# Cached keys transposed by VectorE in 32x32 blocks and scored on 16 array tiles, with a shared ring for keys, values and raw pieces

## The chip, the cores and the metric

The kernel runs on one core of one Trainium2 chip. The metric is the device time of one execution, in microseconds (us). The profile shows TensorE (PE; its weight loads are PEld), VectorE (DVE), ScalarE (ACT), GpSimd (POOL) and the queues of DMA that SP, ACT and GpSimd issue.

## The reference, cut to what matters

One layer of a hybrid decoder runs over a prompt of 256 tokens and over 8 samples of 8 new tokens each, all in float32 with 1024 features. Each sample has 1024 cached tokens in 8 pages of 128, found through a page table. The part that the change touches is the block-sparse attention of the samples: 4 heads of 128 features, blocks of 256 keys, and for each query the three past blocks with the highest mean score, beside the new tokens.

```python
h = x * (1.0 + scale) + shift
rq, rk, rv, rg, mq, mk, mv = project(h, w_in, pos)      # 1024 x 3072 columns, rotary on q and k
...
k_past = cache_k[page_table].reshape(dbs, past_len, h, d)   # 8 x 1024 x 4 x 128
v_past = cache_v[page_table].reshape(dbs, past_len, h, d)
...
gate = einsum("bqhd,bhnd->bqhn", q, kmean)              # mean key of each block of 256
_, top = lax.top_k(gate, 3)                             # of 4 past blocks
logits = einsum("bqhd,bqhsjd->bqhsj", q, ksel) * d ** -0.5
p = softmax(where(mask, logits, -inf))
out = einsum("bqhsj,bqhsjd->bqhd", p, vsel)
...
x = layer_norm(ALPHA * x + gate_a * (concat(retention, out) @ w_o))
x = layer_norm(ALPHA * x + gate_f * (relu(h2 @ w_up) ** 2 @ w_down))
```

## The kernel before

Weights and activations are split into a high and a low part, and a product is three matmuls of such parts. Weights come in pieces of [128, 1024] float32 (512 KB) into a ring of raw tiles, `wr`, of nine slots (`WR`); ScalarE makes the high part and VectorE the low one (`split1`, L162 and L164) into a second ring of eight, `wx`.

The work has three phases. The first, up to about 62 us, computes the modulation of the input by groups of 128 or 256 features (`ada_chunk0`, `pm`, L344) and with it the projection to q and k of the block-sparse heads (`zq`, L398 to L404). Five groups, `CH`, follow each other; the larger ones load four pieces of w_ada (`wa`) and two of w_in (`wi`), and `CUT` says how many units of a group's projection stand ahead of the next group's modulation.

The second phase is made of streams, each a generator whose steps a hand-written list, `SCHEDULE`, puts in an order: `mv`, `qk`, `rv`, `rg` (other columns of the projection), `ga`, `gs`, `gc` (three modulations, L510), `T`, `rT` (transposes of q and k), `K0` and `K1` (scores of the cached keys of samples 0 to 3 and 4 to 7), `V0` and `V1` (their weighted values), `h0` to `h3`, `rs`, `r0`, `r1`, `st`, `sr` (heads of the prompt and retention), `w..` (output projection), `n0` to `n2` (first norm), `ul`, `u0`, `us` (the feed-forward's first block). The list gives priorities; an instruction that waits in the planner's own model can be passed by a later one.

A step of `K0` gathers two pages of keys into a raw tile (`gather`, L267, on GpSimd's queue), transposes each page by heads on TensorE (L543, into the two banks tagged `k`), copies the result to SBUF (`kt`; L549 on ScalarE, L547 on VectorE) and scores pairs of pages with the queries that `pad_queries` has spread over 32 columns per head (L554, four tiles of 128x32 of the array; the scores of a group fill two banks, `psS`). `sample_softmax` chooses blocks and normalizes; `v_steps` loads pages of values, those of SP's queue through `page` (L284).

The third phase, from about 320 us, is the feed-forward by blocks of 512 features (`up`, L1052 to L1054; `down`, L402 to L404 into `acc`) and the second norm.

## Time and profile before

| what | value |
|---|---|
| time, median of 3 runs | 551.0 us (550.35 to 551.13) |
| the profiled execution: its span | 567.5 us |
| PE busy | 517.8 us (91%) |
| DVE, ACT, POOL busy | 311.1, 202.6, 152.8 us |
| data moved | 121.78 MB, mean 215 GB/s |

The span is that of one execution under the profiler, from its first instruction to its last; no other time of that execution is shown. The profiler's execution is longer than the timed ones. Busy time of an engine is the time in which at least one of its instructions of a group runs, so that groups which overlap count twice when added.

### The profile page before, as it was taken

Reading aid. Unit: us, or ns where it says so; the run is one execution under the profiler, and the core shown is the slowest. Engines: PE = TensorE matmul, PEld = TensorE weight load, DVE = VectorE, ACT = ScalarE, POOL = GpSimd, SP = SyncE. Lnnn points to the kernel's source line nnn. Section 1 sums busy time; section 2 is a strip of 40 time slices with the busy share of each in tenths; the row PEclk is TensorE's granted clock in tenths of the full one; section 3 lists DMA queues with packets and bytes.
Section 4 is the critical chain, followed back from the end, with each engine's and each line's share of the span. In section 5 each row is a group of like instructions: output and inputs, shape, how many; then the busy total and the mean of one; then the engine's idle time right before and its main releaser. Section 6 shows DMA issues by size and latency. Waiting matters only on the chain.

```text
span 567.5 us, 8901 instructions
## 1 busy us (share of the span) xinstructions
PE 517.8 (91%) x3346; PEld 398.6 (70%) x3346; DVE 311.1 (55%) x560; ACT 202.6 (36%) x332; POOL 152.8 (27%) x157
## 2 busy tenths in 40 slices
PE   4999999897986999899989888999999999999970
PEld 3777676665654657556658776989888898989860
DVE  1545864371254595573776779253635363636892
ACT  1324434131232533634353643252525252535200
POOL 3000235435572268572611076000000000000041
PEclk9999999999988999999989999899999999999995
DMA  8999978988593478979980645464554655340010
GB/s 219 350 363 371 320 259 284 327 294 323 184 301 127 150 251 287 348 277 317 362 301 2 224 184 164 170 220 153 185 187 167 213 173 175 109 151 1 1 55 37
DMA packets 55364, 121.78 MB, mean 215 GB/s; under 512 B 5321, under 2 KB 18209, under 8 KB 55322
## 3 DMA queue, kind: packets, MB, share of 16 engines
q1 hardware_dynamic: 46954, 97.56, 50.2%
q0 software_dynamic: 7424, 22.75, 11.9%
q10 hardware_dynamic: 944, 0.92, 0.5%
q8 instruction: 26, 0.43, 0.3%
q14 instruction: 16, 0.13, 0.1%
HBM read 117.33 MB, written 3.87 MB: 214 GB/s over the span
## 4 chain that ended last, share of the span: by engine, by line
PE 80%; DVE 7%; another core or an unknown queue 3%; DMA 2%; ACT 2%; issue 2%; POOL 1%; ACTq 0%; SPq 0%; POOLq 0%; DVEq 0%
PE pu L1052 7%; PE pu L1054 6%; PE pu L1053 6%; PE pk L543 5%; PE acc L402 4%; PE acc L403 4%; PE acc L404 4%; PE po L647 3%; PE psS L554 3%; PE acc L399 3%; PE acc L398 3%; PE pm L344 2%; DMA wa<-in_w_ada_dram 2%; PE pw L402 1%
## 5 line engine op out<-in xcount | busy, mean ns | idle before, releaser
L267 POOL DMA_INDIRECT kp<-in_cache_k_dram,idx x64 | 65.9, 1030 | 112.3 <-DMA ga<-in_w_ada_dram 50.9
L996 POOL TENSOR_TENSOR l22r<-l22r,mhalf 64x1 f32<-64x1 f32 x1 | 0.5, 542 | 186.5 <-DVE l22r L995 186.5
L549 ACT ACTIVATE kt<-pk 128x512 f32<-128x512 f32 x48 | 27.9, 596 | 43.7 <-PE pk L543 15.9
L1152 DVE TENSOR_TENSOR usq<-relu 128x320 f32<-128x320 f32 x32 | 17.6, 554 | 45.2 <-ACT relu L1147 44.0
L543 PEld LDWEIGHTS pk<-ident,kp 128*128 128x128 f32 x256 | 28.4, 140 | 18.1 <-issue 12.0
L543 PE MATMUL pk<-ident,kp 128*128 128x128 f32 x256 | 39.0, 280 | 1.1 <-issue 0.8
L1147 ACT ACTIVATE relu<-pu 128x320 f32<-128x320 f32 x28 | 12.1, 432 | 51.6 <-PE pu L1054 51.6
L547 DVE COPY kt<-pk 128x512 f32<-128x512 f32 x16 | 11.0, 690 | 33.0 <-PE pk L543 15.5
L554 PE MATMUL psS<-kt,qpad 128*32 128x256 f32 x256 | 22.4, 388 | 4.7 <-issue 2.4
L184 ACT ACTIVATE uT<-usq 128x320 fp32r<-128x320 f32 x32 | 15.0, 470 | 21.6 <-DVE usq L1152 21.6
L267 POOL DMA_INDIRECT v<-in_cache_v_dram,idx x16 | 18.5, 1157 | 12.1 <-PE po L647 4.5
L187 DVE TENSOR_TENSOR uT<-usq,uT 128x256 fp32r<-128x256 f32 x32 | 15.7, 490 | 7.9 <-ACT uT L184 7.5
L647 PE MATMUL po<-v,PT 128*32 128x512 f32 x128 | 18.1, 601 | 0.0
L344 PE MATMUL pm<-wa,cT 128*32 128x128 f32 x256 | 13.5, 293 | 4.7 <-DMA wa<-in_w_ada_dram 4.7
L344 PEld LDWEIGHTS pm<-wa,cT 128*32 128x32 f32 x256 | 10.0, 117 | 8.5 <-issue 4.5
L1129 POOL TENSOR_TENSOR x<-x,lng 128x512 f32<-128x512 f32 (+1 forms) x6 | 10.1, 1704 | 21.4 <-DMA lng<-in_ln_g_dram 21.4
L554 PEld LDWEIGHTS psS<-kt,qpad 128*32 128x32 f32 x256 | 6.4, 108 | 12.1 <-issue 7.0
L909 POOL TENSOR_TENSOR sg<-sg,rge 128x256 f32<-128x256 f32 (+1 forms) x6 | 4.4, 732 | 23.3 <-DVE rge L907 20.0
L908 DVE RECIPROCAL rge<-rge 128x256 f32<-128x256 f32 (+1 forms) x6 | 10.5, 1743 | 0.1
L1130 POOL TENSOR_TENSOR x<-x,lnb 128x512 f32<-128x512 f32 (+1 forms) x6 | 9.9, 1675 | 0.0
L188 DVE TENSOR_TENSOR uT<-usq,uT 128x64 fp32r<-128x64 f32 x32 | 9.2, 287 | 0.0
L1037 ACT ACTIVATE h2T<-px,shT,scT 128x128 fp32r<-128x128 f32 x16 | 7.0, 458 | 5.2 <-DVE h2f L1038 3.8
(1381 smaller groups left out, 1609.3 us busy)
## 6 DMA issues: line engine op xcount, KB each, us to landing
up<-in_w_up_dram SPq DMA_DIRECT2D x32, 512.0 KB
dn<-in_w_down_dram SPq DMA_DIRECT2D x32, 512.0 KB
v<-in_cache_v_dram SPq DMA_DIRECT2D x48, 256.0 KB
wa<-in_w_ada_dram SPq DMA_DIRECT2D x16, 512.0 KB
wi<-in_w_in_dram SPq DMA_DIRECT2D x8, 512.0 KB
ga<-in_w_ada_dram SPq DMA_DIRECT2D x8, 512.0 KB
gs<-in_w_ada_dram SPq DMA_DIRECT2D x8, 512.0 KB
gc<-in_w_ada_dram SPq DMA_DIRECT2D x8, 512.0 KB
```

The source lines that it names most:

```text
L267: nc.gpsimd.indirect_dma_start(out=dst, out_offset=None, in_=table, in_offset=bass.IndirectOffsetOnAxis(ap=idx[:, b * NPG + s:b * NPG + s ...
L344: pm_last.append(nc.tensor.matmul(pm[32 * j:32 * j + 32, 0:128], cT[:, k, :], wa[c, j // 2, k // per][:, k % per, 128 * i:128 * i + 128], ...
L402: nc.tensor.matmul(acc, hi, wh, start=first, stop=False)
L403: nc.tensor.matmul(acc, lo, wh, start=False, stop=False)
L404: nc.tensor.matmul(acc, hi, wl, start=False, stop=last)
L543: nc.tensor.transpose(pk[:, 128 * h:128 * h + 128], kp[:, s, 128 * h:128 * h + 128], ident)
L549: nc.scalar.activation(dst, src, AF.Copy)
L554: nc.tensor.matmul(psS[pr // 2][32 * h:32 * h + 32, c], qpad[:, h, 4 * g + b, :], kt[:, h, :], start=(b == 0 and pr % 2 == 0), stop=(b == ...
L647: nc.tensor.matmul(po[32 * b:32 * b + 32, :], PT[:, b, s, :], vt[b // 2][:, b % 2], start=False, stop=(s == NPG - 1), skip_group_check=True)
L1052: nc.tensor.matmul(pu[:, toks], wh, hi, start=first and k == ks[0], stop=False)
L1053: nc.tensor.matmul(pu[:, toks], wl, hi, start=False, stop=False)
L1054: nc.tensor.matmul(pu[:, toks], wh, lo, start=False, stop=last and k == ks[-1])
```

## The change

Keys are gathered by four pages into a tile of 1 MB and transposed in place by VectorE, each page of [128, 512] by one instruction in blocks of 32x32. A block then has 32 features in partitions and 32 keys in columns, so that the scores are products over 32 partitions: 16 tiles of the array work side by side, four by groups of keys (each with a bank of its own, four banks instead of two) and four by heads, and four products over blocks of features add up to a head's score. The queries are transposed the same way and copied to four groups of partitions (`pad_queries`, now once for each half of the samples). The softmax first adds the choice of blocks on VectorE into an SBUF tile in the order of keys, then takes one exponential.

Slots change: the raw ring has four instead of nine, a new ring of three tiles of 1 MB (`kv`, opened after the first phase) serves keys, values, and two pieces at a time of the feed-forward's weights and parts; `kt` goes. PSUM's banks are split seven and one instead of six and two. `SCHEDULE` has a new order: keys go with `mv`, `qk`, `rv`, `rg`, and the modulations `ga`, `gs`, `gc` go with the values. The diff, cut to its core:

```diff
-T mv*2 T qk ga T ga mv ga*2 mv qk T mv T qk T mv K0 mv ga mv tb mv K0 ga*2 mv qk mv ga qk mv K0
...
+T*2 K0*3 mv*3 T mv T mv K0 T mv T mv K0*2 mv*2 K0*2 mv*3 tb K0*2 qk*2 ok K0*2 qk*2 ok K0*2 qk*3 K0 qk*2 ov K0 qk*3 ov
+K0 rv*2 K1*3 rv*2 K0 ro rv*2 K1 rv*2 ro K1*2 rv*2 rT K1*2 rv*2 ro K1*2 rT rg*2 K1*2 rg*3 rT K1*2 rg*3 K1 rg*2 K1 rg*2
+K1 sw*2 V0*2 ga rs mx sw V0 ga rs K1 sw h0 V0 ga h1 sw V0 ga*2 r0 sw h0 V0 ga h1 r0 h2 V0 ga sr h3 ga gs r1 h0 V0 gs h2
...
-    WR, WX = 9, 8
+    WR, WX = 4, 8
-        return ps.tile([128, 512], F32, tag=tag, name=nm, bufs={"z": 6, "k": 2}[tag])
+        return ps.tile([128, 512], F32, tag=tag, name=nm, bufs={"z": 7, "k": 1}[tag])
...
+            two = halves(f"{nm}r", self.shape) if kv else ()
+            self.raw = [load(two[i] if i < len(two) else raw_tile(f"{nm}{i}", self.shape),
...
+    def kv_tile(nm):
+        return kvp.tile([128, 4, 512], F32, tag="kv", name=nm, bufs=3)
...
+    qpad = mid.tile([128, 16, 4, 32], F32, tag="qp", name="qpad")
+    def pad_queries(g):
+        if not qtr:
+            qtr[0] = t = mid.tile([64, 512], F32, tag="gny", name="qtr", bufs=1)
+            nc.vector.transpose(t, zs[2][:, 0:512])
+        for r in range(4):
+            v = qpad[32 * r:32 * r + 32]
+            dst = bass.AP(tensor=v.tensor, offset=v.offset, ap=[list(v.ap[0]), [128, 16], [40, 4], [1, 8]])
+            src = qtr[0][32 * g:32 * g + 32].rearrange("p (c b q) -> p c b q", c=16, b=4)
+            if r % 2:
+                nc.gpsimd.tensor_copy(dst, src)
+            else:
+                nc.scalar.activation(dst, src, AF.Copy)
...
-                for h in range(4):
-                    nc.tensor.transpose(pk[:, 128 * h:128 * h + 128], kp[:, s, 128 * h:128 * h + 128], ident)
...
+        def keys(b, half):
+            kt = kv_tile(f"k{g}{b}{half}")
+            for s in range(4):
+                gather(kt[:, s], ck_rows, 4 * g + b, 4 * half + s)
+                nc.vector.transpose(kt[:, s], kt[:, s])
+            return kt
+        def scores(b, half, kt):
+            for j in range(4):
+                for h in range(4):
+                    for r in range(4):
+                        p = slice(32 * r, 32 * r + 32)
+                        nc.tensor.matmul(psS[r][32 * h:32 * h + 32, 128 * half:128 * half + 128],
+                                         qpad[p, 4 * h + j, b, :], kt[p, :, 128 * h + 32 * j:128 * h + 32 * j + 32],
...
+        for r in range(4):
+            v = P[:, 32 * r:32 * r + 32]
+            dst = bass.AP(tensor=v.tensor, offset=v.offset, ap=[list(v.ap[0]), [256, 4], [128, 2], [1, 32]])
+            nc.vector.tensor_tensor(dst, psS[r][:, 0:256].rearrange("p (n s l) -> p n s l", n=4, s=2),
+                                    be[:, :, None, None].to_broadcast([128, 4, 2, 32]), op=ALU.add)
+        nc.scalar.activation(P[:, 0:1024], P[:, 0:1024], AF.Exp, bias=nmx, scale=QS, accum_out=sm[:, 0:1])
...
-                if b % 2 == 0:
-                    vt.append(raw_tile(f"v{g}{s}{b}", [2, 512]))
-                page(vt[b // 2][:, b % 2], 4 * g + b, s)
+                page(vt[:, b], 4 * g + b, s)
...
+        psS = [bank(f"psS{g}{r}") for r in range(4)]
+        if g:
+            pad_queries(1)
...
-        return Weights(wup[0], f"up{blk}", 0, 8, 512 * blk, 512)
+        return Weights(wup[0], f"up{blk}", 0, 8, 512 * blk, 512, kv=True)
...
-            pu = bank("pu", "k")
+            pu = bank("pu", "kz"[m % 2])
```

## Rows read from the trace of the kernel before

**Rows 1.** The page's head and first part: busy us, share, instructions.

```profile
span 567.5 us, 8901 instructions
...
PE 517.8 (91%) x3346; PEld 398.6 (70%) x3346; DVE 311.1 (55%) x560; ACT 202.6 (36%) x332; POOL 152.8 (27%) x157
```

**Rows 2.** Windows by stage: columns as the head line says.

```profile
core 0: us, PE busy (x) PEld busy (x) DVE busy (x) ACT busy (x) POOL busy (x), PEclk, DMA share, GB/s
...
62.00:184.00 122.00, 109.30 (x747) 73.47 (x747) 57.48 (x90) 34.12 (x56) 54.66 (x62) 0.96 0.78 270
184.00:320.00 136.00, 129.31 (x882) 85.98 (x881) 89.03 (x202) 61.53 (x122) 60.04 (x56) 0.99 0.71 246
320.00:567.50 247.50, 225.78 (x1275) 198.17 (x1274) 135.62 (x201) 86.89 (x128) 29.95 (x21) 0.96 0.42 144
```

**Rows 3.** The chain of waits by line, its head.

```profile
by line: PE pu L1052 6.6%; PE pu L1054 6.5%; PE pu L1053 6.3%; PE pk L543 5.4%; PE acc L402 4.0%; PE acc L403 3.9%; PE acc L404 3.9%; PE po L647 3.2%; PE psS L554 2.9%; another core or an unknown queue 2.6%; PE acc L399 2.6%; PE acc L398 2.
```

**Rows 4.** Groups by line: busy us, mean ns; idle before, releaser.

```profile
L543 PE MATMUL pk<-ident,kp 128*128 128x128 f32 x256 | 39.0, 280 | 1.1 <-issue 0.8 <-ACT kt L549 0.3
L549 ACT ACTIVATE kt<-pk 128x512 f32<-128x512 f32 x48 | 27.9, 596 | 43.7 <-PE pk L543 15.9 <-issue 10.6 <-remote 8.1
L554 PE MATMUL psS<-kt,qpad 128*32 128x256 f32 x256 | 22.4, 388 | 4.7 <-issue 2.4 <-DVE kt L547 2.3
...
L547 DVE COPY kt<-pk 128x512 f32<-128x512 f32 x16 | 11.0, 690 | 33.0 <-PE pk L543 15.5 <-remote 8.2 <-issue 5.0
...
L613 DVE TENSOR_SCALAR P<-P,rs 128x1088 f32<-128x1088 f32 x2 | 1.6, 788 | 0.1
```

**Rows 5.** TensorE's waits, 62 to 320 us: total, times, longest.

```profile
PE psS L554 <- issue: 2.4, 3, 1.2
PE psS L554 <- DVE kt L547: 2.3, 2, 1.6
```

**Rows 6.** Timeline of TensorE and its weight loads: start us, us.

```profile
28.23 1.94 PE L344 MATMUL pm<-wa,cT 128*32 128x128 f32 x60
...
100.17 0.16 PEld L554 LDWEIGHTS psS<-kt,qpad 128*32 128x32 f32 x8 [0.17 <-issue]
...
L554 PEld LDWEIGHTS psS<-kt,qpad x256: 106/109/110, 94.1 to 248.8; 128*32 128x32 f32 x128
```

**Rows 7.** The chain of waits, 64 to 90 us: start us, us.

```profile
83.17 1.00 PE gap L510 x16
88.58 0.57 PE gap L510 x8
```

**Rows 8.** Loads and splits: SP's and VectorE's timeline, the chain's DMA.

```profile
22.77 6.76 SPq L174 DMA_DIRECT2D wa<-in_w_ada_dram  x4
...
26.31 1.22 DVE L164 TENSOR_TENSOR wi10l<-wi,wi10h 128x1024 fp32r<-128x1024 f32 x1
...
351.00 3.48 DMA g<-in_w_ada_dram
```

**Rows 9.** Groups by line within 62 to 184 us, TensorE.

```profile
L543 PE MATMUL pk<-ident,kp 128*128 128x128 f32 x132 | 20.5, 280 | 0.8 <-issue 0.8
L554 PE MATMUL psS<-kt,qpad 128*32 128x256 f32 x128 | 11.7, 386 | 3.4 <-DVE kt L547 2.3 <-issue 1.1
...
L510 PE MATMUL gsp<-gs,cT 128*32 128x256 f32 x64 | 5.5, 389 | 0.0
```

**Rows 10.** GpSimd's timeline, two gathers of 256 KB behind each other.

```profile
129.86 0.95 POOL L267 DMA_INDIRECT kp<-in_cache_k_dram,idx  x1 [0.30 <-issue]
131.12 0.95 POOL L267 DMA_INDIRECT kp<-in_cache_k_dram,idx  x1 [0.31 <-issue]
```

**Rows 11.** DMA from 62 to 320 us; windows of 80 and 20 us.

```profile
DMA packets 27258, 66.35 MB, mean 257 GB/s; under 512 B 3390, under 2 KB 5490, under 8 KB 27235
...
60.00:140.00 80.00, 73.97 (x516) 50.74 (x515) 42.53 (x58) 23.33 (x34) 32.83 (x36) 1.00 0.89 311
...
300.00:320.00 20.00, 17.61 (x127) 15.73 (x126) 14.39 (x24) 9.31 (x15) 1.81 (x2) 1.00 0.14 44
```

More of the change, by code (lines that the diff above doesn't have):

```diff
@@ L138, in tile_decoder_step, with __init__ @@
     class Weights:
-        def __init__(self, w, nm, r0, nk, c0, ncol, slots=()):
+        def __init__(self, w, nm, r0, nk, c0, ncol, slots=(), kv=False):
             self.slots = list(slots)
@@ L144, in __init__ @@
             self.nm, self.shape = nm, [self.per, ncol]
-            self.raw = [load(raw_tile(f"{nm}{i}", self.shape), kview(w, r0 + 128 * self.per * i, self.per, c0, ncol))
-                        for i in range(nk // self.per)]
+            two = halves(f"{nm}r", self.shape) if kv else ()
+            self.raw = [load(two[i] if i < len(two) else raw_tile(f"{nm}{i}", self.shape),
+                             kview(w, r0 + 128 * self.per * i, self.per, c0, ncol)) for i in range(nk // self.per)]
             self.parts = {}
@@ L156, in part @@
             def part(x):
-                pl, tag, bufs = self.slots.pop(0) if self.slots else (wpool, "wx", WX)
+                slot = self.slots.pop(0) if self.slots else (wpool, "wx", WX)
+                if callable(slot):
+                    return slot(x)
+                pl, tag, bufs = slot
                 return pl.tile([128] + self.shape, F32R, tag=tag, name=f"{self.nm}{i}{x}", bufs=bufs)
@@ L472, in tile_decoder_step @@
     px1.close()
+    kvp = ctx.enter_context(pool("kvp", side="right"))
     pR = ExitStack()
@@ new lines, in kv_tile, with halves, kv_parts, slot @@
+    def kv_tile(nm):
+        return kvp.tile([128, 4, 512], F32, tag="kv", name=nm, bufs=3)
+    def halves(nm, shape, dtype=F32):
+        v = kvp.tile([128, 2] + shape, dtype, tag="kv", name=nm, bufs=3)
+        return v[:, 0], v[:, 1]
+    def kv_parts(nm, shape):
+        both = {}
+        def slot(x):
+            if not both:
+                both.update(zip("hl", halves(nm, shape, F32R)))
+            return both[x]
+        return [slot, slot]
+    qpad = mid.tile([128, 16, 4, 32], F32, tag="qp", name="qpad")
@@ new lines, in tile_decoder_step @@
+    nc.gpsimd.memset(qpad, 0.0)
+    qtr = {}
+    def pad_queries(g):
[10 more added lines that the diff above has]
+                nc.scalar.activation(dst, src, AF.Copy)
@@ new lines, in k_steps @@
+    def k_steps(g, psS):
+        def keys(b, half):
[11 more added lines that the diff above has]
+                                         qpad[p, 4 * h + j, b, :], kt[p, :, 128 * h + 32 * j:128 * h + 32 * j + 32],
+                                         start=(b + half + j == 0), stop=(b == 3 and half == 1 and j == 3),
+                                         skip_group_check=True)
+        late = []
@@ L560, in k_steps @@
         for b in range(4):
-            for pr in range(4):
-                one, scores = transposes(b, pr)
-                one(0)
+            for half in range(2):
+                late.append((b, half, keys(b, half)))
                 yield
-                if late:
-                    late.pop()()
-                one(1)
-                yield
-                late.append(scores)
-        late.pop()()
-        yield
+                if len(late) > 2:
+                    scores(*late.pop(0))
+                    yield
@@ L573, in tile_decoder_step @@
+        for a in late:
+            scores(*a)
+            yield
     PTs = []
@@ L862, in qk_T @@
             if t == 2:
-                pad_queries()
+                pad_queries(0)
             yield
@@ L912, in values @@
     def values(g):
-        po = bank(f"po{g}", "zk"[g])
+        po = bank(f"po{g}")
         yield from v_steps(g, PTs[g], po)
@@ L918, in scores @@
     def scores(g):
-        psS = [bank(f"psS{g}{hf}") for hf in range(2)]
+        psS = [bank(f"psS{g}{r}") for r in range(4)]
+        if g:
+            pad_queries(1)
         yield from k_steps(g, psS)
@@ L1017, in norm1 @@
         for gq in range(8 // per):
-            px = bank("px2", "k")
+            px = bank("px2")
             for q in range(per):
@@ L1075, in up0_sample @@
     def up0_sample():
-        p = bank("us", "k")
+        p = bank("us")
         for k in range(8):
```

68 lines of the change are left out of this document (18 added, 50 removed).

## The prediction

> **What bounds the kernel now.** I read the page first, then its windows by stage, the chain of waits, and the groups by line. The page's first part shows TensorE busy for 91% of a span of 567.5 us [rows 1]. An average over stages says little, so the windows come next: in 62 to 184 us, TensorE works 109.3 of 122 us while VectorE works 57.5 and the DMA engines 78%; in 184 to 320 us it is 129.3 of 136; from 320 us on the feed-forward alone runs [rows 2]. So in the stage that the change touches, TensorE ends last nearly everywhere, and the other three have room. The chain of waits agrees: it is TensorE's lines throughout, and the keys' transposes (L543) and their scores (L554) hold 5.4% and 2.9% of it [rows 3]. That is 30.6 + 16.5 = 47.1 us of 567.5. The reader should compare this with the groups by line, where the same two lines have 39.0 and 22.4 us busy [rows 4]: overlapping work counts twice there, and I use the chain. TensorE's own waits for this stream add little: 2.4 + 2.3 us [rows 5].
>
> The profiled execution shows its span only, 16.5 us above the median of 551.0. I sum changes of the span and take them off 551.0 one to one.
>
> **What is removed.** The 256 transposes and 256 score records leave the chain: -47.1 us, and the waits for copies of keys -4.7 us. ScalarE loses 48 copies of keys (27.9 us) and VectorE 16 (11.0 us) [rows 4]. Neither stands on the chain as a long piece, so I count nothing for them; what would have shown is VectorE's and ScalarE's slack, and VectorE's is spent below.
>
> **The new scores on TensorE.** The old code has 128 score products and the trace has 256 records [rows 4]: one f32 product is two records. The new code has 1024 products of 32 rows by 32 columns over 128 moving columns, so 2048 records, in 16 batches. Nothing in the trace runs 16 tiles. The nearest row is the modulation's first product, also 32 columns wide and 128 columns long on four tiles: 60 records in 1.94 us, so about 31 ns each [rows 6]. At that price the scores cost 64 us. Is that a limit of the array or of issuing? The batches of 256 columns tell: 16 records take 1.00 us of the chain and 8 take 0.57 [rows 7], so 8 more cost 0.43, 54 ns each. Twice the columns cost nearly twice the time, so it is the array's four tiles and not the issue that sets 31 ns. Sixteen tiles would make it a quarter, 7.8 ns, and 16 us in all; with the fixed 0.14 us of a batch (0.57 - 0.43) 16 times, 18 us. So the ends are 18 and 64 us. I take 24, near the low end, because eight weight loads of about 109 ns each were over after 0.16 us [rows 6], so they started some 7 ns apart; and a third above it, because no stretch shows 128 such records behind each other.
>
> On this the Trainium skill speaks against the change: "TensorEngine Tiling (Array Packing)", section Instruction Overhead, gives each matmul about 60 cycles whatever its columns. By that page, as an estimate, 2048 records cost at least 51 us at 2.4 GHz, and the sum below would end slower than before. The starts 7 ns apart disagree with it for a burst of eight; no row here shows a long run of such records.
>
> **The ring of raw pieces, nine slots to four, in the first 62 us.** The shared ring of keys and values opens only after this phase, so here nothing replaces the five slots. A group of features has four pieces of w_ada and two of w_in. With nine slots SP issues the next group's w_ada at 22.77 us, before TensorE reaches it at 28.23 [rows 6, 8]. With four, the last piece of that group takes the slot of a w_in piece, which comes free with its split, at 26.31 + 1.22 = 27.5 us [rows 8]. A load of 512 KB took 3.48 us where it was waited for [rows 8]: it lands near 31 instead of before 28.2, so some 2.5 us late. The two groups behind repeat the pattern, with part of the delay already absorbed; I count 1.25 us each: +5 us in all. The bounds are 0 (the loads, fewer at once, land sooner) and 4 groups x 3.5 = 14 us.
>
> **VectorE, GpSimd and the queues in the stage of keys and projections.** The new order puts all keys beside mv, qk, rv and rg, and moves the three modulations (5.5 us on TensorE each) behind them. In 62 to 184 us TensorE's work becomes 109.3 less the part of the keys there (20.5 + 11.7) less 3 x 5.5 plus 24: about 85 us [rows 2, 9]. VectorE's becomes 57.5 - 11.0 + 64 transposes. A transpose of 128x512 f32 isn't in the trace; the nearest row is the copy of the same size, 690 ns [rows 4]. The bounds are 0.37 us (half of the 788 ns that one operand of 1088 columns takes within SBUF [rows 4]) and 1.22 us (two operands of 1024 columns [rows 8], were it to run at half speed). At 0.69 they cost 44 us and VectorE comes to 91, plus about 2 for the softmax (four additions of 256 columns at half of 0.69 us, more and shorter reductions). GpSimd issues a gather every 1.25 us [rows 10]: 64 of them are 80 us. So VectorE, at 93, passes TensorE by 8 us, with GpSimd close behind; the transposes stand in VectorE's queue with the splits of the weights, and whoever waits for a late gather there holds up the splits that TensorE needs. I add 8 us for the longer engine and 2 for single steps: the one bank left for transposes, the copies of padded queries ahead of the gathers on GpSimd. +10 us; bounds 0 (at 0.37 us VectorE is at 72, far below TensorE) and, at 1.22 us a transpose, 10 + 34.
>
> **Cross-check by DMA.** From 62 to 320 us 66.35 MB moved, and the best 80 us of that had 311 GB/s [rows 11]. The smaller ring leaves about five slots' worth, 2.6 MB, more to do. 69 MB at 311 GB/s are 222 us; from 67 us on that ends at 289, and about 18 us without loads follow, as at 300 to 320 us now (44 GB/s) [rows 11]. That gives 307 us for the end of the stage instead of 320. The new kernel needs the best rate of the old one throughout, so there is little behind this sum to gain.
>
> **Costed at nothing.** In the feed-forward ten half-megabyte pieces (four slots and three pairs) stand for nine, its TensorE is 225.8 of 247.5 us busy [rows 2], and its loads run far ahead. If that cover fails, a load waited for costs 3.5 us per block. The values come in tiles of four pages instead of two of two, three tiles ahead of their use, with the same products. The order of mixing, heads and retention changes, but not their number of instructions.
>
> **The sum.** -47.1 - 4.7 + 24 + 5 + 10 = -13 us: 551.0 - 13 = 538 us.
>
> **The rivals.**
> - *All of it is gained* (0.13). Scores at 18 us, no queue in front of VectorE, loads keep up: -47.1 - 4.7 + 18 + 5 = -29, so 522 us, and 514 if the ring too costs nothing and the loads run ahead. For it: 16 tiles should run at a quarter of 31 ns. Against it: it needs a DMA rate over 311 GB/s for the whole stage.
> - *TensorE issues too slowly for 16 tiles* (0.20), the case on the other side. Its place is the batch of 128 records, its price 2048 times the distance of two starts. All else as in my sum, the change breaks even where the scores cost 37 us, 18 ns a record, and gets slower from there. At 31 ns, the only sustained row, it is -47.1 - 4.7 + 64 + 5 + 10 = +27, 578 us; the middle is 564. For it: no long run of short records is shown. Against it: the 7 ns between weight loads. The rule of "TensorEngine Tiling (Array Packing)" in the Trainium skill points to this case.
> - *VectorE takes TensorE's place* (0.17). With transposes between 0.69 and 1.22 us, or with gathers late in front of them, the stage is 13 to 34 us longer than I count: 551 to 572 us, middle 560. For it: four resources within 80 to 93 us in one stage and queues that run in order. Against it: VectorE is busy for only 47% of that window now.
> - *The time stays* (0.08). Loads, not TensorE, set the stage's end; with 295 GB/s, a little under the best, 69 MB take 234 us, and 67 + 234 + 18 = 319: 550 us. For it: the old order mixes loads and work more evenly. Against it: DMA is 78% busy and has room.
> - My forecast has 0.42, with a range of its own from 527 to 548 us.
>
> **How the numbers follow.** The likeliest time is 538 us. The range from 514 to 566 leaves out the upper halves of the second and third rivals (0.10 and 0.07) and the lowest corner of the first (0.03). The bound for no change is 0.2%, 1.1 us, about what three runs can tell. Faster gets my forecast, the first rival and a little of the third, 0.57; the same 0.07; slower 0.36.
>
> **What would show it.** Right: the lines L543 and L549 gone; 2048 records of scores with 1.0 to 1.8 us for a batch of 128; transposes on VectorE near 0.69 us; the last group of the first phase some 5 us later; TensorE's waits in the stage now for VectorE or DMA. Wrong: a batch over 2.3 us, transposes over 1 us, the first phase late by over 10 us, or a feed-forward longer than 247 us.

## The result, and the profile after

The changed kernel takes 628.0 us (median of 4 runs, 625.2 to 630.3) against 550.7 us measured beside it: 1.140 times the time before, 95% interval 1.136 to 1.144. The forecast of 538 us was wrong in sign, and no rival came near either: the longest time that I gave one was 578 us. The profiled execution is the longest of the four runs (630.25 us, span 628.5), so profiling need not lengthen an execution, as I had written of the one of before. That one stood 16.5 us above its median; in the groups of runs below the kernel before took medians of 550 to 573 us, and which execution its trace was is not on record. So the spans differ by 61 us and the medians by 77; the stages below account for the 61.

The page's head and first part, after:

```profile
span 628.5 us, 11849 instructions
...
PE 532.6 (85%) x4882; PEld 402.1 (64%) x4882; DVE 344.5 (55%) x626; ACT 178.2 (28%) x277; POOL 160.9 (26%) x161
```

Against [rows 1], TensorE is busy for 15 us more although 256 transposes are gone, and its busy share falls from 91% to 85%. Where the time lies is read from the ends of four things on TensorE: the last product of the first phase (zq), of w_o (pw), of the first block's sample rows (usT), and the end. The windows between them, after, and the one of before for the second:

```profile
core 0: us, PE busy (x) PEld busy (x) DVE busy (x) ACT busy (x) POOL busy (x), PEclk, DMA share, GB/s
76.00:327.00 251.00, 220.79 (x3019) 138.06 (x3018) 155.62 (x314) 56.08 (x93) 110.86 (x113) 0.96 0.76 255
...
327.00:364.00 37.00, 24.79 (x153) 22.46 (x154) 23.27 (x45) 16.73 (x31) 5.15 (x5) 0.77 0.33 108
364.00:628.50 264.50, 230.06 (x1265) 198.41 (x1264) 136.74 (x201) 86.10 (x128) 30.17 (x21) 0.96 0.39 131
```

```profile
62.00:300.00 238.00, 221.00 (x1502) 143.72 (x1502) 132.12 (x269) 86.33 (x164) 112.89 (x117) 0.97 0.79 275
```

| stage | before | after | difference | forecast |
|---|---|---|---|---|
| first phase, to zq | 62 | 76 | +14 | +5 |
| keys, values, to w_o | 238 | 251 | +13 | -18 (-47.1 -4.7 +24 +10) |
| norm and first block | 20 | 37 | +17 | 0 |
| feed-forward | 247 | 264 | +17 | 0 |

No stage gained. In the one with the keys TensorE is busy as long as before, 221 us of both, and idle for 13 us more. The +13 is less sure than the others: three traces of the changed kernel have 251, 249 and 263 us in this stage (a_again and a_again2 below). The last is from a group in which before took 564 us, the level nearest to the trace of before; against it the four differences are +13, +25, +17 and +17. The groups by line that answer to [rows 4], the values' products before, and the chain's loads of the first phase:

```profile
L570 DVE STREAM_TRANSPOSE k<-k 128x512 f32<-128x512 f32 x64 | 43.4, 698 | 35.3 <-DMA k<-in_cache_k_dram,idx 35.1
L578 PE MATMUL psS<-k,qpad 32*32 32x128 f32 x2048 | 40.0, 297 | 6.6 <-issue 2.7 <-ACT qpad L562 2.0 <-POOL qpad L560 1.6
L672 PE MATMUL po<-v,PT 128*32 128x512 f32 x128 | 29.3, 632 | 0.7 <-DMA v<-in_cache_v_dram 0.7
```

```profile
L647 PE MATMUL po<-v,PT 128*32 128x512 f32 x128 | 18.1, 601 | 0.0
```

```profile
30.37 3.45 DMA wa<-in_w_ada_dram
40.42 4.85 DMA wa<-in_w_ada_dram
...
55.70 6.58 DMA wa<-in_w_ada_dram
```

The transposes cost what was expected (698 ns, 43.4 us). The scores hold TensorE for 40.0 us and let it wait 6.6 more, instead of 24. The values' products stretch from 18.1 us to 29.3 with the same 128 records: eight of them took 3.04 us at 230.5, where before eight took 1.07 at 224.8; four of them run side by side when the pages of four samples are there, and one by one when the pages land so. And w_ada's loads, of which only the first stood on the chain of this phase before, are now on it again and again. The head of the chain of waits for the keys' stage, 76 to 327 us:

```profile
by line: PE psS L578 9.7%; DMA k<-in_cache_k_dram,idx 8.5%; issue 7.3%; PE po L672 5.1%; POOL k L270 4.8%; DMA wo<-in_w_o_dram 3.6%; DMA gc<-in_w_ada_dram 2.7%; DMA v<-in_cache_v_dram 2.2%; PE pw L407 2.2%; SPq L286 2.1%; DVE rge L933 2.1%;
```

The loads of keys, w_o, gc and values are on it with 8.5, 3.6, 2.7 and 2.2%. In the same stage before, no load stands among its first lines by name, but 6.2% are an unknown queue, two waits of 7 us; [rows 3] has it too, and the prediction passed over it:

```profile
by line: PE pk L543 12.9%; PE po L647 7.6%; PE psS L554 7.0%; another core or an unknown queue 6.2%; PE pw L402 3.6%; PE pw L404 3.4%; PE pw L403 3.1%; PE pns L826 2.4%; issue 2.1%; PE gap L510 2.0%; PE gcp L510 1.8%; PE mvz L402 1.6%; PE r
```

TensorE's waits over the whole span, after:

```profile
PE pm L347 <- DMA wa<-in_w_ada_dram: 14.1, 9, 2.9
PE g3p L1219 <- DMA g<-in_w_ada_dram: 10.5, 6, 5.1
PE pu L1081 <- POOL h2T L1067: 7.8, 1, 7.8
```

### The profile page after: what moved, and what is told of

The parts are those of the page before. It is cut to its first block, busy times and chain, and to the rows that moved or that the text cites. A ratio compares the mean times of both kernels' runs of the same rounds, so it can differ in the third digit from the quotient of the medians.

```text
span 628.5 us, 11849 instructions
## 1 busy us (share of the span) xinstructions
PE 532.6 (85%) x4882; PEld 402.1 (64%) x4882; DVE 344.5 (55%) x626; ACT 178.2 (28%) x277; POOL 160.9 (26%) x161
## 4 chain that ended last, share of the span: by engine, by line
PE 52%; DVE 15%; DMA 15%; issue 6%; POOL 5%; ACT 3%; SPq 2%; POOLq 0%; DVEq 0%; ACTq 0%
PE pu L1079 6%; PE pu L1081 5%; DMA wa<-in_w_ada_dram 5%; PE pu L1080 5%; PE psS L578 4%; DMA k<-in_cache_k_dram,idx 3%; PE acc L405 3%; PE acc L406 3%; PE acc L407 3%; DMA g<-in_w_ada_dram 3%; POOL k L270 3%; PE acc L402 2%; PE acc L401 2%; PE po L672 2%; PE pm L347 2%
## 5 line engine op out<-in xcount | busy, mean ns | idle before, releaser
L270 POOL DMA_INDIRECT k<-in_cache_k_dram,idx x64 | 69.5, 1086 | 104.8 <-ACT wi41h L165 56.9
L570 DVE STREAM_TRANSPOSE k<-k 128x512 f32<-128x512 f32 x64 | 43.4, 698 | 35.3 <-DMA k<-in_cache_k_dram,idx 35.1
L578 PE MATMUL psS<-k,qpad 32*32 32x128 f32 x2048 | 40.0, 297 | 6.6 <-issue 2.7
L578 PEld LDWEIGHTS psS<-k,qpad 32*32 32x32 f32 x2048 | 29.1, 107 | 17.4 <-issue 7.7
L672 PE MATMUL po<-v,PT 128*32 128x512 f32 x128 | 29.3, 632 | 0.7 <-DMA v<-in_cache_v_dram 0.7
L347 PE MATMUL pm<-wa,cT 128*32 128x128 f32 x256 | 16.2, 341 | 14.1 <-DMA wa<-in_w_ada_dram 14.1
L347 PEld LDWEIGHTS pm<-wa,cT 128*32 128x32 f32 x256 | 11.8, 138 | 19.0 <-DMA wa<-in_w_ada_dram 12.4
L190 DVE TENSOR_TENSOR uT<-usq,uT 128x256 fp32r<-128x256 f32 x32 | 16.8, 524 | 2.6 <-ACT uT L187 1.6
L270 POOL DMA_INDIRECT v<-in_cache_v_dram,idx x16 | 16.0, 997 | 6.4 <-issue 5.1
L1219 PE MATMUL g3p<-g,cT 128*32 128x256 f32 x64 | 6.0, 452 | 10.6 <-DMA g<-in_w_ada_dram 10.5
L672 PEld LDWEIGHTS po<-v,PT 128*32 128x32 f32 x128 | 4.4, 110 | 11.9 <-issue 5.8
```

The costliest lines, as they stand in the source:

```text
L270: nc.gpsimd.indirect_dma_start(out=dst, out_offset=None, in_=table, in_offset=bass.IndirectOffsetOnAxis(ap=idx[:, b * NPG + s:b * NPG + s ...
L347: pm_last.append(nc.tensor.matmul(pm[32 * j:32 * j + 32, 0:128], cT[:, k, :], wa[c, j // 2, k // per][:, k % per, 128 * i:128 * i + 128], ...
L570: nc.vector.transpose(kt[:, s], kt[:, s])
L578: nc.tensor.matmul(psS[r][32 * h:32 * h + 32, 128 * half:128 * half + 128], qpad[p, 4 * h + j, b, :], kt[p, :, 128 * h + 32 * j:128 * h + ...
L672: nc.tensor.matmul(po[32 * b:32 * b + 32, :], PT[:, b, s, :], vt[:, b], start=False, stop=(s == NPG - 1), skip_group_check=True)
```

## The experiments

Three theories were held: A, the raw ring is too small wherever nothing stands for the lost slots; B, the new order of streams; C, the keys' new path (VectorE's transposes, the score records, the tiles that wait for them). In the groups the kernel before took medians of 550 to 573 us (564 and later 550 on one chip), so the ratio to the runs of before in the same group is what is compared; the changed kernel itself gave 1.140, 1.156 (a_again) and 1.145 (a_again2). Stages, in us, are read off each run's trace as above, and are best compared within a group:

| run | ratio, interval | first phase | to w_o | norm, block 1 | feed-forward |
|---|---|---|---|---|---|
| before | 1 | 62 | 238 | 20 | 247 |
| changed | 1.140 [1.136, 1.144] | 76 | 251 | 37 | 264 |
| a_first9 | 1.121 [1.111, 1.131] | 62 | 277 | 35 | 263 |
| a_gown | 1.098 [1.087, 1.109] | 75 | 269 | 37 | 245 |
| a_latet | 1.126 [1.116, 1.136] | 73 | 267 | 35 | 263 |
| b_wr6 | 1.094 [1.083, 1.104] | 63 | 258 | 19 | 276 |
| a_again | 1.156 [1.149, 1.163] | 79 | 249 | 37 | 268 |
| b_keys4 | 1.166 [1.158, 1.173] | 62 | 314 | 19 | 244 |
| a_ul | 1.145 [1.138, 1.153] | 74 | 254 | 35 | 264 |
| a_kv2 | 1.140 [1.134, 1.146] | 62 | 281 | 35 | 250 |
| a_uni | 1.103 [1.091, 1.114] | 65 | 283 | 35 | 244 |
| a_mods | 1.128 [1.115, 1.140] | 75 | 271 | 34 | 262 |
| a_unimods | 1.111 [1.100, 1.121] | 66 | 291 | 34 | 244 |
| a_notr | 1.129 [1.119, 1.139] | 73 | 266 | 35 | 264 |
| b_keys8 | 1.109 [1.101, 1.117] | 62 | 295 | 20 | 245 |
| a_half | 1.119 [1.111, 1.128] | 75 | 253 | 35 | 262 |
| a_nomod | 1.122 [1.113, 1.131] | 77 | 261 | 34 | 264 |
| a_again2 | 1.145 [1.137, 1.153] | 75 | 263 | 37 | 264 |
| b_keys8s | 1.105 [1.100, 1.111] | 63 | 276 | 20 | 245 |
| b_kthold | 1.133 [1.128, 1.137] | 63 | 297 | 20 | 244 |

**First group: the ring's slots, and VectorE's queue.** Five extra slots on the right side until px1, a pool of the first phase, closes:

```diff
+        if extra and len(turn) % 9 < 5:
+            return extra[0].tile([128] + shape, F32, tag="xr", name=nm, bufs=5)
         return wpool.tile([128] + shape, F32, tag="wr", name=nm, bufs=WR)
```

> The changed kernel with nine raw slots again until the end of the first phase (five more in SBUF that is free there), four behind it. Theory A (the small raw ring holds loads back wherever nothing stands for the lost slots): the last product of the first phase comes back from 75.6 to 62-64 us and the total falls by 11 to 14 us, 628 to about 615. Theory B (what is lost is set later, by the order of the streams in the middle, which waits for transfers at its end): the first phase comes back too, but the total falls by less than 5 us. Theory C (the keys' new path through VectorE is the loss): as B.

The first phase is back at 62 us, 11 sooner than in a_latet of the same group; the stage behind takes 10 of them back, and the ratios (1.121, 1.126) can't be told apart. The ring is the cause of the first phase's 14 us, and of no gain by itself: as theory B or C says.

```diff
-        r = {k: load(raw_tile(f"g3{k}", [1, 1024]), kview(...
+        r = {k: load(nat.tile([128, 1, 1024], F32, tag="qkT", name=f"g3{k}", bufs=2), kview(...
```

> The changed kernel with two tiles of their own for the pieces of the last modulation in the feed-forward, so that its four raw slots carry weights alone. Theory A: the feed-forward (from the first block's activation to the end) falls from 264 to 248-252 us, and TensorE's and its weight loads' waits for these pieces (10.5 and 12.4 us) go. Rival: four slots and three pairs are too few for the weights themselves, so the wait only moves to another piece and the feed-forward stays over 258 us. Nothing before 364 us should change.

The feed-forward falls from 263 (a_first9, a_latet) to 245 us, and the total to 628 from 640 and 642. Theory A here; its rival fell.

```diff
-                nc.vector.transpose(kt[:, s], kt[:, s])
...
                 late.append((b, half, keys(b, half)))
+                if len(late) > 1:
+                    turn_keys(late[-2][2])
```

> The changed kernel with the transposes of a tile of keys put one step later in VectorE's queue, behind the gathers of the next tile. Theory C (VectorE stands still for gathers, 35.1 us, with the splits of the weights queued behind it): that wait falls below 10 us, TensorE's waits for split weights fall, and the total falls by 10 to 25 us. Theory A or B: the wait goes, but the total changes by less than 4 us, since the loads behind the four raw slots come no sooner.

VectorE's wait for key loads fell to 26.4 us, not below 10, and the stage did not move: it is 267 us, with 269 in a_gown, which turns the keys in the old place.

```diff
-    WR, WX = 9, 8
+    WR, WX = 6, 8
```

> The kernel before with six raw slots instead of nine, and nothing else. Theory A (slots): the first phase and the feed-forward get longer as in the changed kernel, together 15 to 40 us over 551. Theory B or C (order, keys' path): less than 5 us over 551, since neither is touched.

Three slots less in the kernel before, and nothing else, cost 9.4%: the feed-forward 29 us and the stage of keys and values 20, the first phase only one. First phase and feed-forward together are what theory A forecast; the middle was in no theory. This is the largest effect of one constant in the study, and none of it is about keys.

**Second group: the old path's rival, and three shifts.** The changed kernel again:

> The changed kernel as it is, on the same chip as the others of this group, so that their parts can be held against its own. All theories: 1.14 times the time of the kernel before, whatever this chip's own level; stages at 14 us (first phase), 13 us (to the last product of w_o), 17 us (norm and first block) and 17 us (feed-forward) over the kernel before.

It did, at 1.156, with nearly the same stages. The keys' path alone in the kernel before (the padded queries of the second group are written ahead of the first group's last batch, so that batch is scored with them; the work is the same):

```diff
-            kt = wpool.tile([128, 4, 256], F32, tag="kt", ...
+        def turn(kp, s):
+            nc.vector.transpose(kp[:, s], kp[:, s])
...
+                        kv = kp[p, :, 128 * h + 32 * j:128 * h + 32 * j + 32]
+                        nc.tensor.matmul(pS(r, 32 * h, 64 * pr, 64), qpad[p, 4 * h + j, b, :], kv, ...
```

> The kernel before with the keys' new path alone: pairs of pages transposed by VectorE in the raw ring and scored on 16 tiles, in the old order of streams and with ten raw slots (the room of the transposed keys). As a pair has 64 columns for a tile, its products are 64 columns wide and twice as many (4096 records). Theory A (the small ring is the loss, the keys' path itself gains): 10 to 20 us under the kernel before if a record's price goes by its columns (7.8 ns, 32 us in all), about even if each record costs 15.6 ns whatever its columns (64 us). Theory C (VectorE's queue is the loss): 20 us or more over the kernel before, TensorE waiting for VectorE's splits.

No faster than the changed kernel (641 us against 635), with all of the loss in the stage of keys and values. Its group by line, and three batches of TensorE's timeline:

```profile
L556 PE MATMUL psS<-kp,qpad 32*32 32x64 f32 x4096 | 64.5, 245 | 46.1 <-issue 34.2 <-DVE yr L434 6.8 <-POOL qpad L534 4.8
```

```profile
129.00 1.71 PE L556 MATMUL psS<-kp,qpad 32*32 32x64 f32 x128
...
134.58 1.48 PE L556 MATMUL psS<-kp,qpad 32*32 32x64 f32 x128 [1.35 <-issue]
...
145.88 1.80 PE L556 MATMUL psS<-kp,qpad 32*32 32x64 f32 x112
```

And of the changed kernel, with 128 columns a record:

```profile
109.16 2.25 PE L578 MATMUL psS<-k,qpad 32*32 32x128 f32 x128
...
122.31 2.01 PE L578 MATMUL psS<-k,qpad 32*32 32x128 f32 x128
```

Half the columns make a record only some 20% cheaper (13.6 ns over the three batches, against 16 to 18, the 0.3 us of the last record counted in), so twice the records cost 64.5 us. TensorE also waits 34 us "for issue", that is for nothing that the list of waits names. All but 1.35 us of it lies inside batches, not ahead of them:

```profile
254.52 2.12 PE L556 MATMUL psS<-kp,qpad 32*32 32x64 f32 x128 [2.32 <-issue]
260.72 2.35 PE L556 MATMUL psS<-kp,qpad 32*32 32x64 f32 x128 [4.08 <-issue]
265.54 0.76 PE L556 MATMUL psS<-kp,qpad 32*32 32x64 f32 x36 [2.48 <-issue]
```

These three waits stand 128 records apart, each behind the 77th record of its batch. With their weight loads, 128 records are 256 instructions. The page's third part has queues of the kind "instruction"; the line of one, q8, before and in b_keys4:

```profile
q8 instruction: 26, 0.43, 0.3%
```

```profile
q8 instruction: 54, 0.88, 0.6%
```

TensorE has 2 x 3346 records and weight loads before [rows 1] and 2 x 6930 in b_keys4, so a packet of q8 (16 KB) goes with 256 of its instructions; the changed kernel (38 packets, 2 x 4882) and a_half (30, 2 x 3858) fit too. In b_keys4's trace each of the 13 waits "for issue" over 0.9 us in the scores ended 1.2 to 1.6 us after such a packet had landed. So TensorE most likely waited for its own next instructions there. No run varies this. The changed kernel has such a wait too, inside one batch:

```profile
113.40 1.02 PE L578 MATMUL psS<-k,qpad 32*32 32x128 f32 x59
116.83 1.72 PE L578 MATMUL psS<-k,qpad 32*32 32x128 f32 x69 [2.41 <-issue]
```

```diff
+        yield
         for i in range(4):
             w.split1(i)
...
-w02 w12 w02 w12 wl V1
+w02 w12 w02 w12 wl ul V1
```

> The changed kernel with the four loads of the first block of w_up issued right behind the last loads of w_o, instead of in the middle of the norm (where before has them early too). Theory B (the new order issues loads late): the way from the last product of w_o to the first block's end falls from 37 to 22-26 us and the total by 10 to 15 us. Theory A: no raw slot is free earlier, so less than 4 us.

SyncE's timeline, the loads of the first block: a_ul, the changed kernel, and the kernel before.

```profile
305.43 11.04 SPq L177 DMA_DIRECT2D up<-in_w_up_dram  x5
```

```profile
305.67 11.63 SPq L177 DMA_DIRECT2D up<-in_w_up_dram  x5
```

```profile
263.12 3.11 SPq L174 DMA_DIRECT2D up<-in_w_up_dram  x4
```

The loads are issued no sooner for standing earlier in the program, as theory A said, and the 17 us of the norm don't move.

```diff
-    WR, WX = 4, 8
+    WR, WX = 6, 8
...
-        return kvp.tile([128, 4, 512], F32, tag="kv", name=nm, bufs=3)
+        return kvp.tile([128, 4, 512], F32, tag="kv", name=nm, bufs=2)
...
-                if len(late) > 2:
+                if len(late) > 1:
```

> The changed kernel with two shared tiles instead of three and six raw slots instead of four: the same room, cut another way. Theory A: the first phase gets 6 to 12 us shorter and the feed-forward 10 to 17, while keys and values, with a tile less ahead, lose some: 10 to 25 us less in total. Theory C (gathers come late): the keys' stage gets longer by more than the ring gains, and the total is the same or longer.

Both ends come back (62 and 250 us, 35 us together against a_again) and the stage between loses 32. The ratio, 1.140 against 1.156, keeps little of it.

**Third group: one ring, and the order.** One ring of five pairs, used from the start by all:

```diff
+        if not other:
+            t = wpool.tile([128, 2, 1024], F32, tag="wr", name=nm, bufs=WR)
+            other.extend([t[:, 1], t[:, 0]])
+        return other.pop().rearrange("p (a b) -> p a b", a=shape[0])
```

> The changed kernel with its 40 KB of ring as one: five pairs of half-megabyte slots, from the start on, for raw pieces (two to a pair), keys and values alike. Order of streams and keys' path as in the changed kernel. Theory A (what is lost is lost to the ring's division into four raw slots and three pairs that open late): first phase back to 62 us, feed-forward back to 247, so about 30 us less, and more if the loads in the middle come sooner: 1.08 times the time before, where the changed kernel has 1.14 to 1.16. Theory B (order): the first phase and the feed-forward gain, but the stage between them takes back at least half, as in the run with nine slots in the first phase alone: 1.12 or more.

Both ends again (65 and 244), and again the middle pays, 283 us where a_notr of the same group has 266. The norm stays at 35 with one ring too; in every run with the order of the kernel before it is 20 at most. So those 17 us go with the order, or with PSUM's banks, which are split seven and one in the same runs; the two were not tried apart. The ratio, 1.103, lies between what theory A (1.08) and theory B (1.12 or more) forecast.

```diff
-            self.acc = bank(nm + "p")
+            self.acc = spare[nm]
...
+        for r, nm in enumerate((("ga", "gs"), ("gc",))[g]):
+            spare[nm] = psS[r][:, 256:512]
```

(with ga, gs and gc moved in the schedule, between the steps of K0 and K1)

> The changed kernel with the three modulations back among the projections and keys; their sums stand in the unused columns of the score banks. Ring and keys' path as in the changed kernel. Theory B (the new order puts 33 MB of loads into 106 us behind the keys, which is all that the DMA engines move, and leaves them at 221 GB/s beside the keys): the stage of the values (206 to 312 us) loses 25 us or more, the keys' stage gains less than 10, and the total falls by 15 to 30 us. Theory A (four raw slots): the modulations' pieces, which hold a slot until TensorE has used them, hold up the projections' loads, and the total changes by less than 5 us or rises.

> Both edits together: one ring of five pairs, and the modulations back among projections and keys. If A and B each hold a part, the gains add: 50 to 60 us less than the changed kernel, 1.04 to 1.06 times the time before. If the keys' path itself is the loss (theory C), it stays over 1.10.

Theory B fell for this stage: in a_mods the keys' part takes 168 us and the values' 103, where a_again2 has 143 and 121; what one gains the other loses. The total stays (645 us; 642 in a_notr of the same group), as theory A forecast. And with one ring the two edits don't add up: a_unimods is no faster than a_uni, and over the 1.10 that was to speak for theory C.

```diff
-                nc.vector.transpose(kt[:, s], kt[:, s])
```

> The changed kernel without the 64 transposes on VectorE (the keys are scored as they were loaded; nothing else is left out). Theory C (VectorE, with the transposes in its queue, sets the keys' stage): the stage falls by 20 us or more and with it the total. Theory A or B: TensorE then waits for the gathers itself, and the total falls by less than 8 us.

Nothing: 266 us for the stage without any transposes, with 267 in a_latet on the same chip. The transposes are not what bounds it.

**Fourth group: the price of a record, the loads, the old order.** The new path in the old order, with one ring of five pairs as in a_uni:

```diff
+                kt = wpool.tile([128, 4, 512], F32, tag="wr", name=f"k{g}{b}{half}", bufs=WR)
+                for s in range(4):
+                    gather(kt[:, s], ck_rows, 4 * g + b, 4 * half + s)
                 yield
+                if late:
+                    scores(*late.pop())
+                yield
+                for s in range(2):
+                    nc.vector.transpose(kt[:, s], kt[:, s])
+                yield
```

> The kernel before, in its own order of streams, with the keys' new path in the changed kernel's form (four pages to a tile, transposed by VectorE two steps after the gathers, 2048 records of 128 columns) and one ring of five pairs in place of nine slots. If the order of streams is the loss (theory B), this is faster than the kernel before, 0.97 to 0.99. If the keys' path is the loss (theory C, now in this form: short products cost TensorE 20 ns each with their stalls, and tiles of four pages hold two slots of the ring until they are scored), it stays over 1.05, with the loss between the first phase and the values' end.

With the old order the first phase, the norm and the feed-forward are those of the kernel before. All of the loss, 57 us, is in the stage of keys and values, which by the expectation speaks for theory C.

```diff
-            for j in range(4):
+            for j in (0, 3):
```

> The changed kernel with half of the score products left out (two of four blocks of columns of each head, 1024 records). If TensorE sets the keys' stage, so that every record counts, the total falls by what a record costs: 16 us at 15.6 ns, 20 or more with the stalls between them. If gathers, VectorE or loads set it, by less than 6 us.

15.1 us less than a_again2 for 1024 records, 14.7 ns each: near what was expected if TensorE sets the stage. (Of the 13 us between the two traces only 10 are in the stage of the keys, 10 ns a record, so 14.7 is the upper end.) The groups by line of the two, a_half first:

```profile
L578 PE MATMUL psS<-k,qpad 32*32 32x128 f32 x1024 | 33.5, 304 | 17.1 <-issue 7.2 <-DVE k L570 3.4 <-ACT qpad L562 2.0
```

```profile
L578 PE MATMUL psS<-k,qpad 32*32 32x128 f32 x2048 | 50.3, 312 | 15.3 <-issue 9.3 <-ACT qpad L562 2.0 <-POOL qpad L560 1.5
```

By the record the scores are worth 30 us at most. But half the records still hold TensorE for 33.5 + 17.1 = 50.6 us against 65.6: the other 35 us don't go with their number. They are idle time, 17.1 and 15.3 us, and the pieces into which it breaks a batch, as each piece runs out for 0.3 us behind its last record. In a_again2 many of the pauses are short, and its values' products are as in the first trace:

```profile
117.52 0.42 PE L578 MATMUL psS<-k,qpad 32*32 32x128 f32 x5 [0.31 <-issue]
118.23 0.44 PE L578 MATMUL psS<-k,qpad 32*32 32x128 f32 x5 [0.29 <-issue]
...
L672 PE MATMUL po<-v,PT 128*32 128x512 f32 x128 | 28.9, 618 | 0.0
```

What the short pauses wait for is open. In the first trace of the changed kernel, above, they are few, and the scores hold TensorE for 46.6 us instead of 65.6.

```diff
-            r = load(raw_tile(f"{self.nm}{c}", [nk, self.ncol]), kview(wada[0], ...
+            r = x_t[0][:, None, :]
```

> The changed kernel without the 24 loads of the three modulations behind the keys (12.6 MB; their products run on a tile that is there). Theory B (the values' stage is set by the DMA engines, 308 GB/s): that stage falls from 106 to 75-85 us and the total by 20 to 30. If TensorE or the slots set it: less than 10.

Windows of the values' part, a_nomod first, then a_again2:

```profile
222.00:338.00 116.00, 103.00 (x662) 60.44 (x658) 65.31 (x171) 24.66 (x51) 43.83 (x49) 0.93 0.62 199
```

```profile
218.00:339.00 121.00, 109.20 (x663) 55.66 (x662) 65.63 (x170) 28.21 (x54) 42.27 (x49) 0.99 0.84 292
```

12.6 MB less bring the DMA share from 84% to 62% and save 5 us of 121, far from the 20 to 30 of theory B. The total falls by 11 us (632.6 against 644.0), a little over the mark of 10; this trace is of the longest of its four runs. So the engines of the DMA set little of this part, though 292 GB/s look as if they did.

> The changed kernel once more, on the chip of this group. All theories: 1.12 to 1.16 times the time of the kernel before; what is read from it are its stages.

It took 1.145; its stages are those that a_half and a_nomod are held against.

**Fifth group: slots that keys hold.** b_keys8 with each tile scored sooner:

```diff
                 yield
-                if late:
-                    scores(*late.pop())
                 yield
-                for s in range(2):
+                for s in range(4):
                     nc.vector.transpose(kt[:, s], kt[:, s])
                 yield
+                scores(b, half, kt)
+                yield
```

> As b_keys8, but each tile of keys is transposed two steps after its gathers and scored one step later, so that it holds its two slots for four steps instead of six. If held slots are the loss: SyncE's and GpSimd's waits for scores fall by a third, the stage from the first phase to the values gets 10 to 25 us shorter, and the ratio falls from 1.11 to 1.07-1.09. If TensorE's waits for the keys are the loss, they grow, as it now follows VectorE more closely, and the ratio stays or rises.

SyncE's waits for scores, b_keys8 first:

```profile
SPq L193 <- PE psS L564: 35.2, 5, 15.8
...
SPq L303 <- PE psS L564: 18.7, 5, 6.4
```

```profile
SPq L193 <- PE psS L564: 29.2, 4, 18.3
...
SPq L303 <- PE psS L564: 12.3, 4, 6.1
```

With GpSimd's (35.0 + 15.4 and 16.8 + 8.5) they fall from 104 to 67 us, and the stage from 295 to 276, as expected. The ratio, 1.105 against 1.109, can't be told from the other, and missed its mark; the kernel before itself fell from 564 to 550 us between the two groups, which may be part of the stage's 19 us. It leaves open how much the shorter hold is worth.

```diff
-            kt = wpool.tile([128, 4, 256], F32, tag="kt", name=f"kt{g}{b}{pr}", bufs=2)
+            kt = raw_tile(f"kt{g}{b}{pr}", [4, 256])
...
-    WR, WX = 9, 8
+    WR, WX = 11, 8
```

> The kernel before with its old path of keys, but with the transposed keys in the raw ring (eleven slots in place of nine and two tiles of their own). Engines do the same work. If slots held until the scores are the loss in the new path: 10 us or more over the kernel before, in the stage of keys and values. If not: within 3 us of it.

This settles that held slots cost time in the old order. Every engine does the work of the kernel before, the room is the same, and only the transposed keys stand in the ring until they are scored (and, in the first block, two parts of w_up): 1.133, 59 us of it in the stage of keys and values. Its window, beside the one of before shown above, then SyncE's waits for scores in it:

```profile
63.00:360.00 297.00, 250.12 (x1501) 149.34 (x1500) 134.22 (x269) 87.05 (x163) 113.56 (x117) 0.93 0.65 218
```

```profile
SPq L284 <- PE psS L554: 61.3, 6, 31.1
SPq L174 <- PE psS L554: 21.3, 5, 17.7
```

and SyncE's waits for keys in the kernel before, which has none for scores:

```profile
SPq L174 <- PE pk L543: 26.1, 6, 9.6
...
SPq L284 <- PE pk L543: 12.8, 7, 4.8
```

The same 65 MB take 297 us instead of 238, since a load behind a key in the ring is not issued before that key is scored; TensorE then waits for what was not loaded, 21.6 us for gathers of keys alone:

```profile
PE pk L543 <- DMA kp<-in_cache_k_dram,idx: 21.6, 9, 8.2
```

Of the 59 us 30 are idle time of TensorE; in the other 29 its products take longer, at a mean granted clock of 0.93 instead of 0.97.

## Why the prediction was wrong, step by step

- **Removed, -47.1 - 4.7:** the lines are gone. Right, though the chain that I took it from was not TensorE's throughout.
- **The scores, +24:** mis-sized; they hold TensorE for 40.0 + 6.6 = 46.6 us, nearly all that was removed, and for 65.6 in a_again2. I read 31 ns at four tiles as the array's price and a quarter of it as that of 16 tiles. A further record costs at most 14.7 ns (a_half) and half its columns make it little cheaper (b_keys4), so it is the distance of the starts that sets it. That alone is 30 us, under the 37 us at which my rival of slow issue put the break-even; what goes beyond is time in which TensorE stands still inside batches, and the pieces into which they fall. Neither my sum nor that rival had a term for it. (On the chain, the measure of the -47.1, they hold 9.7% of 251 us, 24.3; but that chain now leaves TensorE for loads, gathers and issue, so I go by TensorE's own time.) "TensorEngine Tiling (Array Packing)" in the Trainium skill, section Instruction Overhead, was the warning. Its 60 cycles, as an estimate 25 ns at 2.4 GHz, are more than a record took in any unbroken batch shown here, 16 to 18 ns. These batches, at 2.0 to 2.3 us, lay between my mark for right and my mark for wrong; the one broken at 113.40 took 5.
- **The ring in the first phase, +5:** it was 14, the upper bound that I gave: I let one group be late by 2.5 us and the two behind it by half of that, but on the chain the waits for w_ada of the last three groups grow (3.5, 4.9 and 6.6 us) instead of being absorbed. The ring as cause is shown by a_first9, a_kv2 and a_uni. That the next stage takes the gain back I had no step for.
- **VectorE and the queues, +10:** no such cost shows. Without the transposes the stage is as long (a_notr), as it is with the transposes later (a_latet). The price of one, 0.69 us, was right, and the rival that VectorE takes TensorE's place fell.
- **Costed at nothing, the feed-forward:** 17 us. I counted ten pieces for nine. But raw and paired slots don't stand for each other: in blocks 1 to 4 the four raw slots serve two pieces of w_up, two of w_down and two of the modulation. With two tiles for the latter the 17 us are gone (a_gown). The test that I named, a feed-forward over 247 us, did show it; b_wr6 has the same in the kernel before, 29 us for three slots.
- **Costed at nothing, the order of mixing:** 17 us in the norm. The loads of the first block of w_up are issued at 306 us, 42 later than before, and their splits fall among the norm's own work on VectorE. TensorE's longest wait there is one of 7.8 us for GpSimd's part of the normed rows, h2T (above). Shown: it comes with the order, or with PSUM's new split (20 us in all runs with the old ones, 34 to 37 with the new, with one ring too). Not shown: which step does it; a_ul was to tell and changed nothing.
- **The cross-check by DMA** is the step that failed most, and with it the loads that "run far ahead". It put the end of the first block at 307 us; it came at 364. I let the loads run at 311 GB/s throughout and asked only how many megabytes were left, not whether a slot was free to issue a load into. In the changed kernel's stage of the keys (76 to 327 us) SyncE, which issues the loads, waited 56 us in all for the splits of five pieces of the projections, 21.0 for one of them, before their slots could be filled again. For scores it waited 7.0 us. Before, its longest wait for a split was 6.5 us:

```profile
SPq L177 <- DVE rv10l L167: 21.0, 1, 21.0
...
SPq L177 <- DVE rg10l L167: 9.6, 1, 9.6
SPq L177 <- DVE qk10l L167: 8.7, 1, 8.7
...
SPq L287 <- PE psS L578: 7.0, 2, 5.5
```

```profile
SPq L174 <- DVE mv10l L164: 6.5, 1, 6.5
```

No run removes these waits alone. The lower rates (253 GB/s with six slots, 218 with keys held in the ring, 255 in the changed kernel) are nearly the same 65 MB over longer stages, and a_nomod shows that the DMA engines were hardly the limit.

So the keys' stage, forecast at -18 us, came out at +13, and at +25 in a_again2. With what was measured the sum reads -51.8 + 46.6 for the scores and + 11.2 for the values' products: +6; for a_again2 it reads -51.8 + 65.6 + 10.8, or +25. But this mixes the chain with busy time. Counted free of overlap, from each start on TensorE to the next, it is -56.3 + 45.6 + 9.7 = -1 for the first trace and -56.3 + 64.5 + 9.1 = +17 for a_again2. So 7 to 14 us of the 13, and up to 8 of the 25, are not accounted for; TensorE's single waits for loads and splits are of that size. What each of the ring's two parts adds there is not separated. That held slots can cost this much is shown in the old order (b_kthold; b_keys8 agrees), not in the changed kernel's own division. And span changes did not carry over one to one: 16 of the 77 us are the excess of the trace of before over its median, which the trace of after does not have.

No version here beats the kernel before. The nearest to it among those with the new path, a_gown, a_uni and b_keys8s, stay 10% slower.

## What to carry to other kernels

A ring of buffers in order is a resource like an engine: before its slots are cut or lent to a tile that lives longer, count for each stage how long each tenant holds its slot, and who issues loads behind it. A busy share and a DMA rate taken from the kernel before hold only while its run-ahead does. And price a short instruction by the distance of its starts in the longest run that the trace has, not by its part of the array; then count how many instructions a batch has.

## What the runs showed of the hardware

- On 16 tiles of 32x32, records of 128 moving columns took 16 to 18 ns each in unbroken batches and of 64 columns 12 to 16, the last record's 0.3 us counted in, though weight loads in a burst of eight started 7 ns apart [rows 6].
- TensorE's instructions come in packets of 16 KB on a queue of their own, 256 to a packet: 26 packets for 6,692 instructions before, 54 for 13,860 in b_keys4. Where 128 short records and their weight loads used a packet up in 2.1 to 2.4 us (b_keys4, 254 to 263 us), TensorE stood still for 2.3 to 4.1 us before the next records. That it waited for the next packet is read from the traces alone.
- Pauses of 0.3 us after every five records, in a_again2, are open.
- VectorE turns 128x512 f32 in 32x32 blocks, in place, in 698 ns: as fast as the copy of that size out of PSUM, 690 ns [rows 4].
